# Other places in the scheduler's order for parts of four mixers, and one for each projection

## The chip, the cores and the metric

The kernel runs on one core of a Trainium2 chip. The time is device microseconds of one execution of the whole program; of several runs the median is given.

## What is computed

One layer of a streaming encoder, on 1024 frames of width 1024. A normalised input goes through one input projection whose columns feed four mixers: attention over chunks (A), HGRN2 (H), RWKV-7 (R) and RG-LRU (L). Their outputs are concatenated, projected, normalised and added to the input; an MLP with squared ReLU follows.

```python
h = rms_norm(x, norm_mix_pre[l])
proj = (h @ w_in[l]).astype(f32)
pa, pb, pc, pd = split_cols(proj, [ATTN_COLS, HGRN_COLS, RWKV_COLS, LRU_COLS])
ya = chunk_attention(qa, ka, va, attn_rel_bias[l])
yb = hgrn2(qb, fb, ib, gb, lb_all[l], hgrn_norm[l].astype(f32))
yc = rwkv7(pc, ...)
yd = rglru(xd, gd, ...)
mix = jnp.concatenate([ya, yb, yc, yd], axis=-1).astype(dt)
x = x + rms_norm(mix @ w_out[l], norm_mix_post[l])
h = rms_norm(x, norm_mlp_pre[l])
ff = jnp.square(jax.nn.relu(h @ mlp_w1[l])) @ mlp_w2[l]
x = x + rms_norm(ff, norm_mlp_post[l])
```

## The kernel before

The frames are worked in two halves of 512 (`hf` 0 and 1). Half 0 takes the mixers in the order R, A, L, H, half 1 in the order R, H, A, L (`ORDER`). After them come the output projection of both halves (`out_mm`, L1049 to L1051), the two residuals, and the MLP (from about 730 us on: L1135 to L1137 and L1384 to L1386).

Every float32 product is made from two parts of each operand (`hi` and `lo`), so a projection of 128 columns (`proj_fm`, L318 to L320) is 24 matmuls of 512 columns: eight pieces of depth, three products each. `proj_tm` (L345 to L347) makes a projection of 256 columns the other way round, with 96 matmuls. Each projection loads its weights on SyncE's queue (`wr`, L167), casts the high part on ScalarE (`wh`, L176) and takes the low part on VectorE (`wl`, L178). There are two buffers each of `wr`, `wh` and `wl`, and two PSUM banks with the tag `fm`; a buffer goes to the tiles of its tag in the order of the code, so the projections keep that order whatever their places are, and each needs that the one two ahead of it has been read. A projection's bank comes free when its reader has run (in R the shift, `pcs`, L360, on VectorE). In this text a projection is named by its columns: W_LO, W_K, W_R, W_V of R, A_K, A_Q, A_V of A, L_X and L_G of L, H_F, H_Q, H_I, H_G of H, with j 0 or 1 for the two blocks of 128.

The parts of the mixers that matter here are:

- R. `Rs`: the shifts and gates of both j (with transposes of v into `pv`, L446, copied to `vt` at L448, and sums into `pbon`, L440); `Rc`: 64 by 64 products of be and al into `plt` (L472), copied to `Ld` and `Lo` by ScalarE (L477, L480); `Ri`: the inverse of the 64 by 64 triangles, first steps of 16 on VectorE, then matmuls of 16 (L529, L537, L539) and of 32 (L551, L562) with copies on ScalarE between them; `Rk`, for four blocks of 128 frames: products (L583), then the chain of states (L614 to L651); `Rn`: the end. The bank pair of `plt` is that of L583's `pcp` too.
- H. `Hf`, `Hq`, `Hv`: gates and values; `Hz`, for j 0 and 1: six levels (L776, with copies under a mask on VectorE, L778); `Hs`: the state (L814 to L819) and the output `po` (L825, L832), added up on VectorE (L835).
- A: `Ap` projections, `Ah` the heads. L: `Lx` and `Lg`.

A scheduler orders the instructions of each engine when the program is compiled. It goes through the program as if it ran, and of the instructions that could start on an engine it takes the one with the lowest number; each engine then runs its instructions in that fixed order. The numbers are a count: each instruction takes the next one. `tc.high_priority(offset=n)` starts its block at the count less n and sets the count back at the block's end, so that a block with a place of its own uses up no numbers. Blocks in blocks add up. `at(...)` opens the block of a part of a mixer with n from `PRIO`, `early_by` that of a whole mixer or of the preparation (`p0`, `p1`).

Of the kernel before, what the change touches and what calls it, by code (L numbers as in the profile page):

```python
# [52 lines left out]
NTAIL = 2  # L53
ORDER = ("RALH", "RHAL")

PRIO = {"p1": 130, "R1": 200, "Rs00": 535, "Ah30": 730, "Rs11": 30, "Hq0": 400, "Ah11": 400, "At1": 400,
# [4 lines left out]
LEVELS = (32, 16, 8, 4, 2, 1)  # L61

VEC = {}
# [25 lines left out]
def body(ctx: ExitStack, tc: tile.TileContext, A: dict, out: bass.AP, dbg=None, stop_after=None):  # L89
# [11 lines left out]
    def at(*key):  # L101

        sec.close()
        n = PRIO.get("".join(map(str, key)), 0)
        if n:
            sec.enter_context(tc.high_priority(offset=n))
# [5 lines left out]
    def bank(name, tag="pa"):  # L112
        return psp.tile([P, 512], F32, tag=tag, name=nm(name), bufs=PB[tag])
# [29 lines left out]
    def load_consts():  # L143
        for name, shape in (("cmask", [P, 512]), ("masks", [P, 3 * CH]), ("bones", [P, 2]), ("rkw", [P, 4]),
                            ("lo2", [P, 256]), ("lnw", [P, 256]), ("lnb", [P, 256]), ("hnorm", [P, 256]),
                            ("lgate", [P, 512]), ("lam", [P, 2])):
            consts[name] = load(name, shape, keep)
        lm = ub("lm")[:, 0:6 * CH]
        nc.sync.dma_start(lm, A["lmask"])
        lm8 = keep.tile([P, 6 * CH], mybir.dt.uint8, tag="lm8", name="lm8")  # L150
        V.tensor_copy(lm8[:], lm)
        consts["lmask"] = lm8

        om = keep.tile([P, 25], F32, tag="om", name="om")

        V.tensor_scalar(om[:, 0:7], vecs[:, VEC["mu"]:VEC["mu"] + 7], -1.0, 1.0, MULT, ADD)
        V.tensor_scalar(om[:, 9:11], vecs[:, VEC["k_k"]:VEC["k_k"] + 2], -1.0, None, MULT)

        for i, name in ((13, "bx"), (15, "k_k"), (17, "k_a"), (21, "w0"), (23, "a0")):
            V.tensor_scalar(om[:, i:i + 2], vecs[:, VEC[name]:VEC[name] + 2], 0.5, None, MULT)  # L160
        V.tensor_scalar(om[:, 19:21], om[:, 17:19], -1.0, 1.0, MULT, ADD)
        consts["om"] = om
# [7 lines left out]
    def wload(src, eng=None):  # L170
        return wparts(wraw(src), eng)
# [87 lines left out]
    def spread(hf):  # L259

        rb = bank("rb")
        for t in range(4):
            dg = small.tile([P, P], F32, tag="pdg", name=nm("pdg"))
            V.tensor_scalar(dg[:], ident[:], rs_[hf][:, t:t + 1], None, MULT)
            T.matmul(rb[:, t * P:(t + 1) * P], ones[:], dg[:], start=True, stop=True)
        S.copy(rb_[hf][:], rb[:])

    def prep0():
        nc.sync.dma_start(vecs[:], A["vecs"])
        cols = W_LO, W_K  # L270
        hs, xs, ws = [], [], []
        for k in range(NK):
            xs.append(xload(0, k, lambda s, d, name: hp.tile(s, d, tag="hl", name=name, bufs=NLO)))
            if k < 2:
                ws.append(wraw(wsrc[cols[k]][0]))
        nc.sync.dma_start(ident[:], A["ident"])
        for k, h in enumerate(xs):
            hs.append(parts_in(0, k, h))
            if k < 2:
                early[cols[k]] = wparts(ws[k], (V, G)[k])  # L280
        stats(0)
        proj_pair(hs, *cols)
        spread(0)
        return hs

    def stats(hf):

        ss = small.tile([P, 4, 2], F32, tag="prs", name=nm("prs"))
        for t in range(4):
            for n in range(2):  # L290
                xt = ub("xsq")
                nc.sync.dma_start(xt[:], A["x"][hf * TH + t * P:hf * TH + (t + 1) * P, n * 512:(n + 1) * 512])
                S.activation(xt[:], xt[:], AF.Square, accum_out=ss[:, t, n:n + 1])
        V.tensor_tensor(rs_[hf][:], ss[:, :, 0], ss[:, :, 1], ADD)
        inv_rms(rs_[hf][:], rs_[hf])

    def prep1():
        hs = []
        for k in range(NK):
            h = xload(1, k, lambda s, d, name: hp.tile(s, d, tag="hl", name=name, bufs=NLO))  # L300
            hs.append(parts_in(1, k, h))
        return hs
# [12 lines left out]
    def mm_in(ps, wh, wl, hs, k):  # L315
        hi, lo = hs[k]
        ks = slice(k * P, (k + 1) * P)
        T.matmul(ps[:], wh[:, ks], hi[:], start=(k == 0), stop=False, skip_group_check=True)  # L318
        T.matmul(ps[:], wl[:, ks], hi[:], start=False, stop=False, skip_group_check=True)  # L319
        T.matmul(ps[:], wh[:, ks], lo[:], start=False, stop=(k == NK - 1), skip_group_check=True)  # L320

    def proj_fm(hs, col):

        if col in done:
            return done.pop(col)
        wh, wl = wload(wsrc[col][0])
        ps = bank("fm", "fm")
        for k in range(NK):
            mm_in(ps, wh, wl, hs, k)
        return ps  # L330

    def proj_tm(hs, col):

        pss = [bank("tm", "fm") for _ in range(2)]
        for i, src in enumerate(wsrc[col]):
            wh, wl = wload(src)
            for t in range(4):
                tsl = slice(t * P, (t + 1) * P)
                o = pss[t // 2][:, 256 * (t % 2):256 * (t % 2) + 256]
                for kk in range(4):  # L340
                    k = i * 4 + kk
                    hi, lo = hs[k]
                    cs = slice(kk * 256, (kk + 1) * 256)
                    last = k == NK - 1
                    T.matmul(o, hi[:, tsl], wh[:, cs], start=(k == 0 and t % 2 == 0), stop=False, skip_group_check=True)  # L345
                    T.matmul(o, lo[:, tsl], wh[:, cs], start=False, stop=False, skip_group_check=True)  # L346
                    T.matmul(o, hi[:, tsl], wl[:, cs], start=False, stop=last, skip_group_check=True)  # L347
        return [pss[t // 2][:, 256 * (t % 2):256 * (t % 2) + 256] for t in range(4)]
# [23 lines left out]
    def rwkv(hf, hs):  # L372
        om = consts["om"]
        lo2 = consts["lo2"]
        at("Rs", hf)

        xlo = rwkv_shift(hf, proj_fm(hs, W_LO), 6, "xlo")
        lot = u("lot")
        S.activation(lot[0:32, :], xlo[0:32, :], AF.Tanh)
# [550 lines left out]
    def lru_setup():  # L930

        lam = consts["lam"][:]
        w = [keep.tile([P, 2], F32, name=f"lw{i}") for i in range(4)]
        S.activation(w[0][:], lam, AF.Abs)
        S.activation(w[0][:], w[0][:], AF.Exp, scale=-1.0)
        V.tensor_scalar(w[1][:], w[0][:], 2.0, None, ADD)
        V.reciprocal(w[1][:], w[1][:])
        V.tensor_tensor(w[0][:], w[0][:], w[1][:], MULT)
        V.tensor_tensor(w[1][:], w[0][:], w[0][:], MULT)
        V.memset(w[2][:], 1.0 / 17)  # L940
        for n in (15, 13, 11, 9, 7, 5, 3, 1):
            V.tensor_tensor(w[2][:], w[2][:], w[1][:], MULT)
            V.tensor_scalar(w[2][:], w[2][:], 1.0 / n, None, ADD)
        V.tensor_tensor(w[2][:], w[2][:], w[0][:], MULT)
        V.tensor_scalar(w[3][:], lam, -1.0, 0.0, MULT, MAX)
        V.tensor_scalar(w[2][:], w[2][:], 8.0, None, MULT)
        V.scalar_tensor_tensor(sp8[:, 0:2], w[3][:], 4.0, w[2][:], MULT, ADD)
        V.tensor_scalar(sp8[:, 2:4], sp8[:, 0:2], -1.0, None, MULT)
# [541 lines left out]
    def early_by(n):  # L1490
        return tc.high_priority(offset=n) if n else ExitStack()

    for hf in range(2):
        if hf == 0:
            with early_by(PRIO.get("p0", 0)):
                hs = prep0()
            load_consts()
            for z in zqs + Sbds:
                G.memset(z[:], 0.0)
        else:  # L1500
            with early_by(PRIO.get("p1", 0)):
                hs = prep1()
        for f in ORDER[hf]:
            with early_by(PRIO.get(f + str(hf), 0)):
                {"R": rwkv, "A": attention, "L": lru, "H": hgrn}[f](hf, hs)
                at()
            if f == "R" and hf == 0:
                at("st")
                lru_setup()
                stats(1)  # L1510
                spread(1)
                at()
        if stop_after == f"mix{hf}":
            return
# [84 lines left out]
```

## Time and profile before

| | us |
|---|---|
| median of 3 runs | 1353.74 (1353.53 to 1358.21) |
| profiled execution, time | 1363.41 |
| profiled execution, span | 1361.4 |
| PE busy | 1287.6 (95% of the span) |
| PE weight loads busy | 1017.0 (75%) |
| VectorE busy | 861.6 (63%) |
| ScalarE busy | 662.2 (49%) |
| GpSimd busy | 81.2 (6%) |
| granted TensorE clock, mean | 0.963 of full speed |

The span runs from the first to the last instruction. "Busy" of PE holds time in which the array stands between two matmuls, so 95% doesn't say that it worked at its peak. The granted clock is 1.00 at 2.4 GHz and 0.50 at 1.2 GHz; a stretch between them holds some of both.

### The profile page before, as it was taken

Reading aid. Unit: us, or ns where it says so; the run is one execution under the profiler, and the core shown is the slowest. Engines: PE = TensorE matmul, PEld = TensorE weight load, DVE = VectorE, ACT = ScalarE, POOL = GpSimd, SP = SyncE. Lnnn points to the kernel's source line nnn. Section 1 sums busy time; section 2 is a strip of 40 time slices with the busy share of each in tenths; the row PEclk is TensorE's granted clock in tenths of the full one; section 3 lists DMA queues with packets and bytes.
Section 4 is the critical chain, followed back from the end, with each engine's and each line's share of the span. In section 5 each row is a group of like instructions: output and inputs, shape, how many; then the busy total and the mean of one; then the engine's idle time right before and its main releaser. Section 6 shows DMA issues by size and latency. Waiting matters only on the chain. (4 is left out here: it accounts for less than half of the span.)

```text
span 1361.4 us, 21277 instructions
## 1 busy us (share of the span) xinstructions
PE 1287.6 (95%) x8168; PEld 1017.0 (75%) x8168; DVE 861.6 (63%) x1575; ACT 662.2 (49%) x1171; POOL 81.2 (6%) x123
## 2 busy tenths in 40 slices
PE   6999999899988999999799899999999999999997
PEld 4677778666677777767588678888887888888886
DVE  5653645687463567685648889786774545554884
ACT  6634535565154344574658445444543533433441
POOL 1000010223001123000000000000000000000000
PEclk9998999999688999999899899999998999999999
DMA  8222012311023011235632698787656976556761
GB/s 293 101 92 74 33 61 82 111 61 61 32 81 79 18 39 66 80 122 179 244 126 103 224 312 275 244 267 255 225 174 219 367 253 199 186 187 192 271 231 62
DMA packets 101157, 213.72 MB, mean 157 GB/s; under 512 B 25280, under 2 KB 28992, under 8 KB 101056
## 3 DMA queue, kind: packets, MB, share of 16 engines
q1 hardware_dynamic: 101056, 212.37, 46.1%
q8 instruction: 64, 1.05, 0.3%
q14 instruction: 37, 0.30, 0.1%
HBM read 157.02 MB, written 55.31 MB: 156 GB/s over the span
## 5 line engine op out<-in xcount | busy, mean ns | idle before, releaser
L1384 PE MATMUL q<-b,a 128*128 128x512 f32 x448 | 175.9, 394 | 2.4 <-ACT b L1368 2.4
L1385 PE MATMUL q<-b,a 128*128 128x512 f32 x448 | 176.6, 394 | 0.9 <-DVE b L1369 0.9
L1386 PE MATMUL q<-b,a 128*128 128x512 f32 x448 | 176.3, 393 | 0.0
L318 PE MATMUL fm<-hh,wh 128*128 128x512 f32 x304 | 132.9, 438 | 10.2 <-ACT wh L176 7.6
L319 PE MATMUL fm<-hh,wl 128*128 128x512 f32 x304 | 131.2, 433 | 0.9 <-DVE wl L178 0.9
L320 PE MATMUL fm<-hl,wh 128*128 128x512 f32 x304 | 130.1, 430 | 0.0
L178 DVE TENSOR_TENSOR wl<-wr,wh 128x1024 fp32r<-128x1024 f32 x66 | 82.4, 1249 | 48.4 <-ACT wh L176 47.7
L176 ACT CAST wh<-wr 128x1024 fp32r<-128x1024 f32 x66 | 68.9, 1045 | 87.6 <-PE fm L320 64.9
L1384 PEld LDWEIGHTS q<-b,a 128*128 128x128 f32 x448 | 84.4, 189 | 21.4 <-ACT b L1368 2.8
L1385 PEld LDWEIGHTS q<-b,a 128*128 128x128 f32 x448 | 84.7, 189 | 20.4 <-DVE b L1369 1.7
L1386 PEld LDWEIGHTS q<-b,a 128*128 128x128 f32 x448 | 84.8, 189 | 18.9
L318 PEld LDWEIGHTS fm<-hh,wh 128*128 128x128 f32 x304 | 61.3, 202 | 24.0 <-ACT wh L176 8.3
L1369 DVE TENSOR_TENSOR b<-wb,b 128x1024 fp32r<-128x1024 f32 x32 | 39.1, 1223 | 60.4 <-ACT b L1368 60.2
L319 PEld LDWEIGHTS fm<-hh,wl 128*128 128x128 f32 x304 | 61.3, 202 | 17.4 <-issue 4.3
L320 PEld LDWEIGHTS fm<-hl,wh 128*128 128x128 f32 x304 | 60.8, 200 | 15.0 <-issue 2.6
L1368 ACT CAST b<-wb 128x1024 fp32r<-128x1024 f32 x32 | 33.5, 1048 | 78.7 <-PE q L1385 63.7
L1369 DVE TENSOR_TENSOR a<-ha,a 128x1024 fp32r<-128x1024 f32 x56 | 68.2, 1218 | 5.5 <-ACT a L1368 5.4
L1119 ACT CAST s<-w 128x512 fp32r<-128x512 f32 x64 | 39.3, 619 | 62.4 <-DVE w L1200 16.1
L1369 DVE TENSOR_TENSOR b<-wt,b 128x1024 fp32r<-128x1024 f32 x24 | 29.4, 1224 | 55.9 <-ACT b L1368 55.9
L1368 ACT CAST a<-ha 128x1024 fp32r<-128x1024 f32 x56 | 58.5, 1045 | 7.7 <-DMA ha<-hx 7.7
L1368 ACT CAST b<-wt 128x1024 fp32r<-128x1024 f32 x24 | 25.2, 1049 | 73.5 <-PE q L1385 73.5
L346 PE MATMUL tm<-wh,hl 128*128 128x256 f32 x192 | 55.2, 288 | 0.0
(1082 smaller groups left out, 3045.2 us busy)
## 6 DMA issues: line engine op xcount, KB each, us to landing
ha<-hx SPq DMA_DIRECT2D x56, 512.0 KB, 4.6
wr<-in_win_dram SPq DMA_DIRECT2D x50, 512.0 KB, 3.3
w<-in_w_dram SPq DMA_DIRECT2D x36, 512.0 KB, 5.2
wb<-in_w_dram SPq DMA_DIRECT2D x32, 512.0 KB, 6.6
wt<-tx SPq DMA_DIRECT2D x32, 512.0 KB, 3.7
w2s<-in_w_dram SPq DMA_DIRECT2D x48, 256.0 KB, 4.0
tx<-w2s SPq DMA_DIRECT2D x48, 256.0 KB, 2.4
hx<-h SPq DMA_DIRECT2D x48, 256.0 KB, 3.2
```

Of the source, the lines that this page charges most:

```text
L176: S.copy(hi[:], raw[:])
L178: V.tensor_tensor(lo[:], raw[:], hi[:].bitcast(F32), SUB)
L318: T.matmul(ps[:], wh[:, ks], hi[:], start=(k == 0), stop=False, skip_group_check=True)
L319: T.matmul(ps[:], wl[:, ks], hi[:], start=False, stop=False, skip_group_check=True)
L320: T.matmul(ps[:], wh[:, ks], lo[:], start=False, stop=(k == NK - 1), skip_group_check=True)
L346: T.matmul(o, lo[:, tsl], wh[:, cs], start=False, stop=False, skip_group_check=True)
L1119: S.copy(t[:, 0, :], src)
L1368: S.copy(h_, r[:])
L1369: V.tensor_tensor(l_, r[:], h_.bitcast(F32), SUB)
L1384: T.matmul(o, ah[:, i, tsl], bh[:, i, :], start=start, stop=False, skip_group_check=True)
L1385: T.matmul(o, ah[:, i, tsl], bl[:, i, :], start=False, stop=False, skip_group_check=True)
L1386: T.matmul(o, al[:, i, tsl], bh[:, i, :], start=False, stop=stop, skip_group_check=True)
```

## The change

The table `PRIO` gets other values, and every projection gets a place of its own, under the key "p", its first column, "." and the half.

```diff
+PRIO = {"A0": 30, "Ah01": 400, "Ah10": 100, "Ah11": 400, "Ah20": 60, "Ah21": 260, "Ah30": 730, "At0": 700, "At1": 400,
+        "Hq0": 400, "Hz00": 400, "Hz01": 160, "L0": 30, "L1": 11, "Lg00": 600, "Lg11": 15, "Lx0": 485, "Oh0": 200,
+        "Ol0": 40, "Ol1": 400, "Or0": 400, "Or1": 350, "Pm": 629, "R1": 200, "Ri1": 535, "Rk00": 200, "Rk01": 125,
+        "Rk11": 85, "Rk31": 405, "Rn1": 600, "Rs0": 160, "Rs00": 600, "Rs10": 60, "Rs11": 30, "p0": 800, "p0.1": 196,
+        "p1": 65, "p1536.1": 10, "p2048.1": 10, "p2304.0": 800, "p2688.0": 445, "st": 320}
...
+    half_of = [0]
+
+    def sooner(*key):
+        n = PRIO.get("".join(map(str, key)), 0)
+        return tc.high_priority(offset=n) if n else ExitStack()
+
     def proj_fm(hs, col):
+        with sooner("p", col, ".", half_of[0]):
+            return proj_fm_(hs, col)
+
+    def proj_tm(hs, col):
+        with sooner("p", col, ".", half_of[0]):
+            return proj_tm_(hs, col)
...
     for hf in range(2):
+        half_of[0] = hf
```

The values that differ: p0 none to 800, p1 130 to 65, Rs0 none to 160, Rs00 535 to 600, Rk00 none to 200, st 400 to 320, Lg00 60 to 600, Hs10 30 to none, Hs11 45 to none, Rk01 100 to 125, Rk31 415 to 405, Rn1 200 to 600, L1 none to 11, Ol0 none to 40, Or1 370 to 350; of projections W_V j 0 of half 0 (p2304.0, 800), L_X j 0 of half 0 (p2688.0, 445), A_Q j 0 of half 1 (p0.1, 196), W_K j 0 and H_G of half 1 (p2048.1 and p1536.1, 10 each). No part of the kernel uses "Pm", "At0" or "At1".

What this makes of the numbers, counted along the code by the rule above:

| block | number before | number after |
|---|---|---|
| preparation of half 0 | 15 to 122 | -785 to -678 |
| W_R j 0, half 0 | -345 to -319 | -527 to -501 |
| W_V j 0, half 0 | -307 to -281 | -1289 to -1263 |
| L_X j 1, half 0 | 506 to 532 | 256 to 282 |
| L_G j 0, half 0 | 885 to 911 | 122 to 148 |
| Ri, half 0, its L537 and L539 | 329 to 424 | 212 to 307 |
| Ri, half 0, its L551 and L562 | 431 to 496 | 314 to 379 |
| Hz j 1, half 0 | 1347 to 1426 | 1124 to 1203 |
| Rs j 1, half 1, from its k to its end | 1365 to 1498 | 1190 to 1323 |
| of it the transposes of v, L446 | 1493 to 1496 | 1318 to 1321 |
| Rc, half 1, its copies L477 and L480 | 1427 to 1432 | 1252 to 1257 |
| Hs j 1, half 0, its L825 and L832 | 1433 to 1456 | 1240 to 1263 |
| H_F j 0, half 1, its matmuls | 1430 to 1453 | 1282 to 1305 |
| H_F j 1, half 1, its matmuls | 1460 to 1483 | 1312 to 1335 |
| A_Q j 0, half 1 | 1970 to 1996 | 1602 to 1628 |
| A_K j 0, half 1 | 1942 to 1968 | 1770 to 1796 |
| output projection, half 0 | 2405 to 2638 | 2046 to 2279 |

The matrices, the instructions and their buffers are the same.

## Rows read from the trace of the kernel before

**Rows 1.** The page: TensorE's busy time, and its busy and clock tenths by slice.

```profile
PE 1287.6 (95%) x8168; PEld 1017.0 (75%) x8168; DVE 861.6 (63%) x1575; ACT 662.2 (49%) x1171; POOL 81.2 (6%) x123
PE   6999999899988999999799899999999999999997
PEclk9998999999688999999899899999998999999999
```

**Rows 2.** Stretches by window, start:end first; the columns are in the first row.

```profile
core 0: us, PE busy (x) PEld busy (x) DVE busy (x) ACT busy (x) POOL busy (x), PEclk, DMA share, GB/s
336.00:348.00 12.00, 8.79 (x54) 7.01 (x53) 11.73 (x24) 3.02 (x4) 0.75 (x1) 1.00 0.09 24
476.00:510.00 34.00, 34.00 (x308) 25.30 (x307) 23.42 (x68) 15.43 (x35) 8.31 (x10) 1.00 0.10 34
```

**Rows 3.** Timeline of TensorE, 301 to 373 us: start, duration, line, tiles, count.

```profile
301.14 1.10 PE L825 MATMUL po<-iv,att 128*128 128x64 f32 x8
...
354.21 0.79 PE L320 MATMUL fm<-hl,wh 128*128 128x512 f32 x1
...
361.43 0.79 PE L319 MATMUL fm<-hh,wl 128*128 128x512 f32 x1
362.16 0.47 PE L832 MATMUL po<-sall,qe 64*64 64x64 f32 x2
362.56 0.79 PE L320 MATMUL fm<-hl,wh 128*128 128x512 f32 x1
...
370.75 0.50 PE L318 MATMUL fm<-hh,wh 128*128 128x512 f32 x1
371.19 0.32 PE L832 MATMUL po<-sall,qe 64*64 64x64 f32 x2
371.44 0.50 PE L319 MATMUL fm<-hh,wl 128*128 128x512 f32 x1
...
372.56 0.45 PE L832 MATMUL po<-sall,qe 64*64 64x64 f32 x8
```

**Rows 4.** Stretches by window around that place and behind it.

```profile
350.00:370.00 20.00, 20.00 (x123) 14.17 (x124) 5.02 (x13) 1.89 (x4) 3.10 (x4) 0.50 0.08 27
380.00:385.00 5.00, 0.80 (x17) 0.56 (x19) 2.42 (x3) 4.87 (x9) 0.59 (x2) 0.86 0.16 18
385.00:391.00 6.00, 6.00 (x61) 4.88 (x53) 0.00 (x0) 5.91 (x8) 0.00 (x0) 0.55 0.52 162
394.00:399.00 5.00, 5.00 (x24) 4.14 (x23) 4.79 (x11) 3.42 (x5) 0.00 (x0) 1.00 0.00 0
```

**Rows 5.** Timeline of ScalarE, 354 to 384 us; in brackets idle time before, and its releaser.

```profile
372.67 1.05 ACT L176 CAST wh<-wr 128x1024 fp32r<-128x1024 f32 x1 [17.97 <-PE fm L320]
...
380.58 0.58 ACT L448 COPY vt<-pv 128x512 f32<-128x512 f32 x1
381.06 2.37 ACT L477 COPY Ld<-plt 32x512 f32<-32x512 f32 x4
```

**Rows 6.** Timeline of TensorE, 379 to 385 us.

```profile
379.44 0.60 PE L446 MATMUL pv<-ident,xv 128*128 128x128 f32 x4
...
384.67 0.71 PE L583 MATMUL pcp<-xk,sg 64*64 64x64 f32 x16 [4.21 <-ACT Lo L480]
```

**Rows 7.** Timeline of SyncE's queue, VectorE and TensorE at the start.

```profile
8.23 0.33 SPq L167 DMA_DIRECT2D wr<-in_win_dram  x1
...
24.68 2.35 DVE L178 TENSOR_TENSOR wl<-wr,wh 128x1024 fp32r<-128x1024 f32 x2
...
27.28 0.49 PE L265 MATMUL rb<-pdg,ones 128*128 128x128 f32 x2 [1.98 <-DVE pdg L264]
29.17 0.80 PE L318 MATMUL fm<-hh,wh 128*128 128x512 f32 x1 [1.40 <-DVE pcs L360]
```

**Rows 8.** Stretches by window in R of half 0, during Ri's small matmuls.

```profile
120.00:124.00 4.00, 3.67 (x150) 2.18 (x147) 2.15 (x3) 3.64 (x8) 0.00 (x0) 0.60 0.03 6
124.00:128.00 4.00, 2.67 (x62) 1.66 (x56) 1.22 (x3) 1.84 (x4) 0.95 (x1) 0.50 0.35 131
```

More of the change, by code (lines that the diff above doesn't have):

```diff
@@ L54 @@
 ORDER = ("RALH", "RHAL")
-PRIO = {"p1": 130, "R1": 200, "Rs00": 535, "Ah30": 730, "Rs11": 30, "Hq0": 400, "Ah11": 400, "At1": 400,
[4 rows of a table removed]
+PRIO = {"A0": 30, "Ah01": 400, "Ah10": 100, "Ah11": 400, "Ah20": 60, "Ah21": 260, "Ah30": 730, "At0": 700, "At1": 400,
[4 rows of a table added]
 LEVELS = (32, 16, 8, 4, 2, 1)
@@ L320, in mm_in, with proj_fm_ @@
         T.matmul(ps[:], wh[:, ks], lo[:], start=False, stop=(k == NK - 1), skip_group_check=True)
+    half_of = [0]
+    def sooner(*key):
+        n = PRIO.get("".join(map(str, key)), 0)
+        return tc.high_priority(offset=n) if n else ExitStack()
     def proj_fm(hs, col):
+        with sooner("p", col, ".", half_of[0]):
[3 more added lines that the diff above has]
+            return proj_tm_(hs, col)
+    def proj_fm_(hs, col):
         if col in done:
@@ L330, in proj_fm, with proj_tm_ @@
         return ps
-    def proj_tm(hs, col):
+    def proj_tm_(hs, col):
         pss = [bank("tm", "fm") for _ in range(2)]
```

4 rows, old and new, of the table PRIO are left out of this document.

## The prediction, made before the changed kernel had run

> **What bounds the kernel now.** I read first the page's busy times and its slices. TensorE is busy 1287.6 us, 95% of the span [rows 1]: no change of order can win more than what TensorE idles (74 us), what it loses at a lower clock, and what it loses between matmuls while it counts as busy. All other engines have spare time in every stage. So each edit is asked one thing: does TensorE stand still, run at the lower clock, or change between kinds of matmul less often? The slices say where this can be. From slice 20 on (the output projection and the MLP, about 690 us on) nothing that the change moves is left, but for the order of the loads in front of them. The mixers are the first 17 slices (0 to 590 us), and the clock there is low in slices 3, 10, 11 and 12, worst in 10, at 340 to 374 us, with 0.6 [rows 1]. In most others TensorE is full, as from 476 to 510, 34.00 of 34 us [rows 2]; there an order can only move work about.
>
> I read next the timeline of TensorE in the worst slice. It shows H_F j 0 of half 1 (512 columns, `fm`) taken in turn with the output of Hs j 1 of half 0 (L825, L832): one big, one pair of small ones, one big [rows 3]. From 350 to 370 us TensorE is busy for all 20 us and has the clock of 1.2 GHz, 0.50 [rows 4]. A turn takes 1.13 us there (361.43 to 362.56) and 0.69 us still at full clock (370.75 to 371.44) [rows 3], where big matmuls in a row take about 5.00 / 22, 0.22 us each [rows 4] (24 are in that window, two cut by its ends). The reason is in the table of places: 1430 to 1453 and 1433 to 1456 are the same numbers, and the scheduler merges the two by number.
>
> Third, ScalarE's timeline behind it: it stands idle 17.97 us in front of a cast that waits for H_F's last matmul, and the copies of `plt`, whose matmuls were done at 352, come at 381.06, behind the copy of `pv` (L448) [rows 5]. The transposes that feed that copy run at 379.44, when H_F j 1 is through, and TensorE then idles 4.21 us for `Lo` [rows 6].
>
> **The change part by part.** The shifts in the table come from blocks that no longer use up numbers: 108 of the preparation, 9 of Rs, 106 of Rk (223 in all for what follows in half 0), while Hs j 1 lost its own place and uses up its 75 again (so H of half 1 moves by 148), and 27 of W_K make R's later parts move by 175.
>
> *Hs j 1 against H_F (the main term).* After: 1240 to 1263 against 1282 to 1305. The small ones come first whenever they can run, and H_F runs in one piece beside their waits. From 354.21 to the end of L832 at about 372.9 are 18.7 us [rows 3], with 22 big matmuls, 16 of L825 and 28 of L832. In pieces and at full clock: 22 x 0.22 = 4.8; 16 of L825 at 1.10 per 8 [rows 3], 2.2; 28 of L832 at 0.45 per 8 [rows 3], 1.6; together 8.6 us, so 10.1 less. Its lower end: if the clock stays at 1.2 GHz through, 17.2 us, 1.5 less. After the next idle time, with dense work behind it, 6.0 us had a clock of 0.55 and the stretch from 394 had 1.00 again [rows 4]; that is the nearest row, and such a stretch costs 2.7 us. 10.1 - 2.7: I take 7, between 1.5 and 10.1.
>
> The row shows that a turn of big and small costs more than both in rows of their own. The Trainium skill ("TensorEngine Tiling (Array Packing)", Key Properties) says why: a change of the tiling mode drains TensorE. This trace agrees (0.69 us a turn at full clock, against 0.22 and a share of 0.45 per 8); the sum is the same with or without the rule, but the rule holds as well where the change puts new numbers side by side, which is the second rival.
>
> *The transposes of v.* Numbers 1318 to 1321 now fall into H_F j 1's 1312 to 1335, where they were behind it: about 18 of its 24 matmuls come later, 18 x 0.22 = 4 us earlier for `pv`, and for the `plt` copies behind it. What goes is at most the idle 4.21 us [rows 6] and the slow clock after it, 6 x 0.45 = 2.7 [rows 4], 6.9 together; at least nothing, if the casts of the next projections still stand first on ScalarE. Next late would then be H_Q's cast (L176), which waits for H_F's buffer. I take 2.5.
>
> *The start.* The preparation now comes before the loads and splits of W_R. Before, W_R's load stood ahead of five of the loads of x (8.23 us), two splits on VectorE ran for 2.35 us between `pdg` products, TensorE waited 1.98 us for the last of these and 1.40 us more for `pcs` [rows 7]. W_V, with the lowest number of all, can't pass W_R: buffers go in code order. It can still take VectorE with its one split, 1.2 us. So between 0 and 3.4; I take 2.5. W_V's matmuls will run ahead of W_R's, a swap that pays for itself.
>
> *L_G j 0 and L_X j 1 against Ri.* They go from behind Ri's matmuls to in front of them (122 to 148, 256 to 282). Before, L_G filled the chain of Rk instead. Ri's steps lose 1.66 us idle and, at clocks of 0.60 and 0.50, 1.6 + 2.0 us of speed in 120 to 128 [rows 8]. If the fills cover that, up to 5.3 us less; if L_X takes turns with L537 and L539 (numbers 259 to 282 within 212 to 307), 24 turns of 0.4 us (0.69 less 0.22 less the small one's 0.06) [rows 3, 4], 9.6 us more. L_X's weights were not split in time for this before, and buffers come no sooner now. I take 0.
>
> *At nothing.* p1: the splits of x for half 1 have numbers above Hz and the heads as before; only Hz j 1 has come to stand before them, and it can't start until Hs has given back its bank; cost between 0 and 1. The whole of R in half 1 stands 48 to 75 places later against H of half 0; VectorE is full there (11.73 of 12 us) [rows 2], its sum is unchanged, but readers of banks (L360) wait longer: between -3 and +5, taken at 0, because TensorE has those same projections to do behind it. A_Q before A_K in half 1, st, Rk00, Rk01, Rk31, Rn1: they run where TensorE is full [rows 2], which hides a swap; without that cover each is worth one ScalarE copy and its wait, under 1 us. Ol0, Or1, L1 and the output projection's lower numbers: its operands need buffers that the last projection of L holds, so only splits move, -2 to +2.
>
> Sum: 7 + 2.5 + 2.5 + 0 = 12 us less. In the profiled execution, 1363.4 - 12 = 1351.4; that execution is 9.7 us above the median of the runs, so I set the 12 us against the median: 1353.7 - 12 = **1342 us**.
>
> **The rivals.** *Given back.* The turns go, but the copies of `plt` still stand behind casts on ScalarE and the chain of R starts no earlier; TensorE then runs out of projections sooner and idles longer before L583. Only the start is won: 1353.7 - 2.5 = 1351. For it: ScalarE's 18 us of idle before one cast [rows 5]. Against it: `pv` does move ahead.
>
> *The turns move.* L_X's matmuls merge with L537 and L539 as Hs did with H_F: 1342 + 9.6 = 1352. For it: overlapping numbers. Against it: the weights come late. By the page named above it would happen wherever two tile sizes alternate.
>
> *Slower: Ri runs bare.* If L_G's block ends before the first L537 and L_X is spent in turns with the small ones, the waits of Ri's later steps have no projection left but L_G j 1. From 118 to 138 us, 20 us before, 8 were L_X at mixed clock; 12 remain bare, less 5.3 of L_G j 1, 6.7 idle, and some 3 us of slow clock behind, as in [rows 4]. With the 9.6 of turns: 1342 + 19.3 = 1361. It decides at the point where L_G j 1's first matmul comes after L562. For it: L_G now has a lower number than all of Ri from L537 on. Against it: buffers free up in time for L_G j 1 if L_G is done early.
>
> **How the numbers follow.** Forecast (1342) 0.60, given back (1351) 0.17, turns move (1352) 0.11, slower (1361) 0.12. The measurement of this kernel can tell about 0.5%, 6.8 us, from no change: the first is faster (0.60), the two middle ones are the same (0.28), the last is slower (0.12). The forecast's own bounds: 10.1 + 6.9 + 3.4 + 5.3 = 25.7 us less at best, though not all at once, so 24 is the low end, 1330; the high end takes in both middle cases with some room, 1358. Left out are the slower case (most of its 0.12) and a few hundredths below.
>
> **What would show it.** Right: L825 and L832 in runs of eight and more with no `fm` between them; a clock near 1 within some us of 350; L446 before H_F j 1's end and the idle time before half 1's first L583 under 2 us; the first L318 after `rb` about 2.5 us earlier. Wrong: new turns of L318 to L320 with L537 or L539; a longer idle time before L551, L562 or L583; the same span with the gain of 350 to 373 gone by the start of the output projection.

## The result and the profile after

The changed kernel takes 1333.92 us (1332.13 to 1337.04), the kernel before 1355.97 in the same runs: ratio 0.983, 95% interval 0.980 to 0.986, 22 us less. The profiled execution took 1337.04 us, with a span of 1335.2. In the code of after, the lines behind `proj_fm` stand 14 higher: L360 is L374, L446 is L460, L583 is L597, L825 and L832 are L839 and L846, L1049 is L1063, L1167 is L1181.

The page after, beside [rows 1]: busy times, and TensorE's busy and clock tenths in 40 slices.

```profile
PE 1269.3 (95%) x8168; PEld 1006.3 (75%) x8168; DVE 858.5 (64%) x1575; ACT 665.6 (50%) x1173; POOL 81.9 (6%) x123
PE   6899999899998999989997999999998999999997
PEclk9998999999997999999998999999998999999999
```

TensorE has the same 8168 matmuls and is busy 18.3 us less; it idles 7.9 us less (65.9 for 73.8). The low clock of slices 10 and 11 is gone; slice 12 has 0.7 for 0.8. Windows around H_F of half 1 (start:end; PE, PEld, DVE, ACT, POOL busy; granted clock; DMA), beside [rows 4]:

```profile
330.00:345.00 15.00, 14.59 (x108) 10.51 (x106) 11.43 (x26) 5.12 (x9) 1.49 (x3) 1.00 0.11 38
345.00:361.00 16.00, 15.41 (x141) 12.62 (x140) 8.91 (x15) 8.61 (x15) 3.08 (x4) 1.00 0.33 87
```

The clock is 1.00 throughout. The turns have not all gone: half of L846's matmuls of Hs j 1 still take turns, now with the last projection of R (W_V j 1) instead of H_F (TensorE's timeline: start, duration, line, tiles, count):

```profile
340.32 0.33 PE L846 MATMUL po<-sall,qe 64*64 64x64 f32 x2
340.57 0.51 PE L318 MATMUL fm<-hh,wh 128*128 128x512 f32 x1
341.01 0.33 PE L846 MATMUL po<-sall,qe 64*64 64x64 f32 x2
```

From Hs j 1's first output to its last there are 12 changes between `fm` and `po`, where before has 34. The transposes of v, beside [rows 6], and the first product of Rk behind them (in brackets idle time before and its releaser):

```profile
355.10 0.27 PE L460 MATMUL pv<-ident,xv 128*128 128x128 f32 x1
...
361.04 0.46 PE L597 MATMUL pcp<-xk,sg 64*64 64x64 f32 x16 [0.51 <-ACT Lo L494]
```

They run within H_F j 1 (which ends at 360.3), and the idle time of 4.21 us is 0.51.

Where the time went, by stage, from the first and last matmuls of named tiles in one profiled execution each (us; the last three columns are kernels of the next section):

| stage | before | after | prep_first | three_parts | wv_back |
|---|---|---|---|---|---|
| to W_R's first matmul | 29.2 | 27.3 | 27.6 | 26.9 | 26.2 |
| to the end of A_V, half 0 | 90.4 | 91.1 | 88.1 | 88.0 | 88.0 |
| to the end of H_G, half 0 | 127.6 | 125.2 | 127.3 | 126.8 | 123.8 |
| to the end of H_F j 1, half 1, and Hs j 1, half 0 | 133.3 | 116.7 | 126.6 | 120.8 | 118.1 |
| to the end of the output projection, half 0 | 268.5 | 272.2 | 268.8 | 271.8 | 268.8 |
| to its end, half 1 | 60.3 | 50.7 | 58.6 | 50.2 | 50.7 |

So of the 26 us between the two profiled executions, 16.6 lie where the prediction looked, and 9.6 in the output projection of half 1, where it saw 2 at most; the other stages cancel. Behind it both take 652 us. Each stage holds its execution's share of slow clock: before and prep_first have the same order in the fourth stage and differ by 6.7 us, and after_again, which is after once more, takes 53.1 us for the last stage, not 50.7.

**The clock as a second result.** Every execution has its mean granted clock. Within a kernel, a hundredth of it goes with 10.7 us (the slope over the 180 executions compared here, each kernel's mean taken out; an expectation below was written with 11.7, from fewer of them). It lets the part of a difference that comes with the clock be set aside. Time at a clock of 0.975, and the mean clock:

| kernel | executions | median | mean clock (range) | at 0.975 |
|---|---|---|---|---|
| before | 75 | 1355.7 | 0.968 (0.960 to 0.974) | 1348.9 |
| hs10_sooner | 12 | 1354.2 | 0.969 (0.961 to 0.977) | 1347.8 |
| prep_first | 12 | 1352.5 | 0.969 (0.963 to 0.972) | 1346.0 |
| r_later | 12 | 1350.8 | 0.970 (0.966 to 0.972) | 1344.7 |
| hs10_plain | 6 | 1341.7 | 0.973 (0.964 to 0.976) | 1342.4 |
| prep_and_hs10 | 6 | 1342.6 | 0.973 (0.965 to 0.981) | 1339.7 |
| three_parts | 6 | 1338.3 | 0.979 (0.976 to 0.982) | 1342.0 |
| after, after_again | 10 | 1333.4 | 0.978 (0.974 to 0.979) | 1336.7 |
| shift_back | 11 | 1346.8 | 0.972 (0.963 to 0.979) | 1346.2 |
| lg_back | 6 | 1332.4 | 0.979 (0.975 to 0.981) | 1337.6 |
| out_back | 6 | 1336.6 | 0.976 (0.971 to 0.980) | 1338.4 |
| wv_back | 6 | 1328.5 | 0.981 (0.978 to 0.984) | 1334.6 |
| wv_back_r_later | 12 | 1350.0 | 0.970 (0.963 to 0.976) | 1344.5 |

The last column has a standard error of 0.2 us for before and 0.3 to 0.7 for the others. One execution each of hs10_plain and shift_back, in a slower state of the chip, is left out. Of the 22 us, 12 are there at the same clock, and 0.010 of clock is the other 11.

### The profile page after: what moved, and what is told of

The parts are those of the page before. It is cut to its first block, busy times and chain, and to the rows that moved or that the text cites. A ratio compares the mean times of both kernels' runs of the same rounds, so it can differ in the third digit from the quotient of the medians.

```text
span 1335.2 us, 21293 instructions
## 1 busy us (share of the span) xinstructions
PE 1269.3 (95%) x8168; PEld 1006.3 (75%) x8168; DVE 858.5 (64%) x1575; ACT 665.6 (50%) x1173; POOL 81.9 (6%) x123
## 5 line engine op out<-in xcount | busy, mean ns | idle before, releaser
L318 PE MATMUL fm<-hh,wh 128*128 128x512 f32 x304 | 129.2, 426 | 13.4 <-ACT wh L176 8.9
L319 PE MATMUL fm<-hh,wl 128*128 128x512 f32 x304 | 126.9, 418 | 0.9 <-DVE wl L178 0.9
L320 PE MATMUL fm<-hl,wh 128*128 128x512 f32 x304 | 125.7, 416 | 0.0
L1382 ACT CAST a<-ha 128x1024 fp32r<-128x1024 f32 x56 | 58.6, 1046 | 8.8 <-DMA ha<-hx 8.8
L361 PE MATMUL tm<-wl,hh 128*128 128x256 f32 x192 | 56.0, 292 | 0.6 <-DVE wl L178 0.6
```

The costliest lines, as they stand in the source:

```text
L1382: S.copy(h_, r[:])
```

## The experiments

All compare with runs of the kernel before on the same chip. A number near 1 is the ratio of the times, with its 95% interval in brackets; "in the medians" and "at the same clock" are the columns of the table above. Two theories stood at the outset. "Turns": H_F in turns with the output of Hs j 1 makes the slow clock of 350 to 370 us. "What runs beside Hz j 1": TensorE idles just ahead, the clock falls there, and the turns only lie in the slow stretch.

**hs10_sooner: the tie alone.**

```diff
-"Hs10": 30
+"Hs10": 60
```

> The kernel before with one number of the table changed: Hs j 1 of half 0 gets 60 for 30. Its block uses up no numbers either way, so all else keeps its number; only the tie of L825 and L832 with H_F j 0 of half 1 is gone (1403 to 1426 against 1430 to 1453). Theory 'turns': TensorE changes between big and small matmuls less often and the slow clock of 350 to 370 us goes with it: 5 to 8 us less than before, so about 1349 against 1356. Theory 'what runs beside Hz j 1': the clock falls because TensorE idles beside Hz j 1 just ahead (325 to 349 us), and the turns only come to lie in a stretch that is slow anyway; then the time moves by less than 2 us.

Measured: 0.9989 (0.9968 to 1.0010), 1.1 us less at the same clock. "Turns" falls: of 36 changes between H_F's matmuls and L825 or L832 in the trace of before 13 are left, and hardly anything comes of it. Something else did come with the tie: in this kernel's profile the output projection of half 1 takes 51.0 us with 2.1 idle, as short as in after. Windows of before (first line) and of this kernel where TensorE idles in it:

```profile
660.00:680.00 20.00, 11.78 (x42) 8.40 (x41) 9.87 (x17) 10.87 (x21) 0.00 (x0) 0.76 0.64 229
650.00:660.00 10.00, 9.37 (x44) 7.22 (x43) 5.78 (x11) 7.29 (x19) 0.00 (x0) 1.00 0.95 349
660.00:670.00 10.00, 8.52 (x40) 6.31 (x39) 5.89 (x8) 7.78 (x15) 0.00 (x0) 1.00 0.36 116
```

**prep_first: the start alone.**

```diff
+"p0": 800
```

> The kernel before with p0 800 alone: the preparation of half 0 goes ahead of the loads of R's first projections; all later numbers fall by the same 108, so nothing else changes place. By the prediction 2.5 us less (0 to 3.4), by the traces of before and after 1.5 to 2 us less at W_R's first matmul; a rival: what is won at the start is lost at the next wait, time as before.

Measured: 0.9968 (0.9944 to 0.9991), 3.6 us less in the medians, 2.9 at the same clock: the start as predicted. Its profile says more than was asked. From R's first shifts on, TensorE's instructions stand in the order of before, all the turns with them. Windows, and three lines of TensorE's timeline:

```profile
346.00:352.00 6.00, 6.00 (x34) 4.71 (x31) 2.81 (x10) 1.36 (x3) 0.73 (x2) 0.50 0.00 0
352.00:362.00 10.00, 10.00 (x56) 6.35 (x54) 0.42 (x1) 0.21 (x1) 0.00 (x0) 0.99 0.00 0
```

```profile
352.56 0.33 PE L832 MATMUL po<-sall,qe 64*64 64x64 f32 x2
352.81 0.49 PE L320 MATMUL fm<-hl,wh 128*128 128x512 f32 x1
353.24 0.33 PE L832 MATMUL po<-sall,qe 64*64 64x64 f32 x2
```

The turns run at full clock for 10 us, where before had 0.50 up to 370 us [rows 4]. The clock came back in their midst, so they don't hold it down; the same order took 126.6 us for this stage instead of 133.3. A turn costs 0.68 us at full clock here, as in [rows 3].

**hs10_plain: tie and shift.** Without a place, Hs j 1 uses up 75 numbers, and R of half 1 stands that much later against H of half 0.

```diff
-"Hs10": 30
```

> The kernel before with one entry of the table taken out: Hs j 1 of half 0 has no place of its own and uses up its 75 numbers, so that the tie is gone and R of half 1 with all behind it stands 75 numbers later against H of half 0. Theory 'turns': the same 5 to 8 us less as with the tie alone taken away. Theory 'what runs beside Hz j 1': H of half 0 runs ahead of R of half 1, whose projections are left to fill the waits of Hz j 1, the clock doesn't fall there: 10 to 15 us less than before, and clearly less than with the tie alone taken away.

Measured: 0.9906 (0.9871 to 0.9940), 14 us less in the medians, 6.5 at the same clock, 5.4 more than the tie alone: the number of the second theory. Its reason, that the clock doesn't fall there, did not come: in its profile the clock stays low for longer than in before's (the windows of hs10_plain below).

**r_later: the shift alone, the tie's numbers kept.**

```diff
-"R1": 200
+"R1": 125
```

> The kernel before with the place of R in half 1 at 125 for 200: all of that R stands 75 numbers later against H of half 0, and since its block uses up no numbers nothing else moves; L825 and L832 keep the numbers of H_F j 0 of half 1. Theory 'what runs beside Hz j 1': R's projections are left for the waits of Hz j 1, about 4.5 us less than before at the same granted clock, as the step from the tie alone to tie and shift gave. Rival 'turns': no gain beyond that of fewer turns, 1 to 1.5 us at the same clock.

Measured: 0.9960 (0.9941 to 0.9980), 4.1 us less in the medians and 4.2 at the same clock. The order of R of half 1 against H of half 0 has a price of its own: the turns with H_F are gone here too, but the tie alone gave only 1.1. But the clock is no better (0.970), and its profile shows why that is another matter:

```profile
330.00:337.00 7.00, 2.97 (x16) 2.75 (x16) 5.98 (x9) 0.83 (x3) 0.00 (x0) 0.84 0.23 78
337.00:367.00 30.00, 29.95 (x146) 22.44 (x147) 12.12 (x28) 9.24 (x16) 2.72 (x4) 0.53 0.05 18
```

TensorE idles 4.03 of 7 us beside the last steps of Hz j 1, and then works for 30 us without a break at 0.53.

**shift_back: the changed kernel with the 75 numbers back.**

```diff
+"Hs10": 30
```

> The changed kernel with Hs j 1 of half 0 back at place 30: its 75 numbers are not used up, R of half 1 and all behind it stand 75 numbers sooner again against H of half 0, as before the change. L825 and L832 have the numbers of H_F j 0 again, but H_F runs ahead of them in the compiled order, so that there are few turns (12 changes, with H_F j 1, for 37 before). Theory 'turns': within 3 us of the changed kernel (1334). Theory 'what runs beside Hz j 1': 8 to 12 us above the changed kernel, about 1344, with idle time beside Hz j 1 and a slow clock behind it.

Measured: 1346.84 us, 0.9954 (0.9923 to 0.9984): 13 us above the changed kernel in the medians, 9.5 at the same clock, and the clock down to 0.972. One number undoes more than half of the gain, with few turns in sight. "Turns" had said within 3 us. But the sign that the second theory gave is missing. In two windows of its profile around Hz j 1:

```profile
320.00:330.00 10.00, 9.56 (x49) 6.99 (x50) 9.92 (x22) 5.70 (x11) 2.15 (x3) 1.00 0.01 2
330.00:340.00 10.00, 7.91 (x93) 6.12 (x92) 9.23 (x20) 2.92 (x4) 1.20 (x2) 0.95 0.10 36
```

From Hz j 1's first matmul to Hs j 1's first output TensorE idles 2.5 us, no more than in after (2.8), and the clock is low for 3.4 us up to H_F's end. In the profile the loss lies in the stage up to the end of H_F and Hs j 1 (6.5 us more than after) and in the two stages behind it (1.8 and 2.1). So the number came true, and not by the idle time beside Hz j 1.

**prep_and_hs10 and three_parts: do the parts add up?**

```diff
+"p0": 800
-"Hs10": 30
```

> The kernel before with two of the changes: p0 800, and Hs j 1 of half 0 without a place. If the parts add up, 3.1 (p0) and 5.8 (Hs j 1) us less at the same granted clock, about 1339.7 at 0.975 against 1337 of the changed kernel. Theory 'the clock follows these two': its granted clock is 0.976 or more, as that of the changed kernel, and the median 1336 to 1340. Rival 'the clock has other causes': 0.971 as with Hs j 1 alone, and a median of 1343 to 1346.

Measured: 0.9913 (0.9881 to 0.9946). At the same clock they add up: 2.9 and 6.5 make 9.4, and 1348.9 less 1339.7 is 9.2. The clock doesn't come with them: 0.965 to 0.981, three of six at 0.969 or less. The third part, with the place in the code of after:

```diff
+"p0": 800, "p2048.1": 10
-"Hs10": 30
```

> The kernel before with three of the changes: p0 800, Hs j 1 of half 0 without a place, and the place 10 for W_K j 0 of half 1, which makes R's later parts stand 27 numbers sooner, so 48 instead of 75 later than before. With the first two alone, the last steps of Hz j 1 have no projection beside them (its last 12 matmuls stand in a row, 3.5 to 4 us idle), the clock spreads from 0.965 to 0.981 and the median is 1342.7. With the third, six matmuls of R's last projection (W_LO's j 1, columns 2432) come between them, and the order up to H_F is that of the changed kernel. Theory 'the idle time beside Hz j 1 decides whether the clock falls there': granted clock 0.975 to 0.980 in nearly all runs, median 1335 to 1338, within 3 us of the changed kernel. Rival 'the clock has other causes': clock spread as with two parts, median 1340 to 1343.

(The columns 2432 are W_V j 1; the expectation misnames them.) Measured: 1338.32 us, 0.9851 (0.9815 to 0.9888), and a clock of 0.976 to 0.982 in all six. The median is just above the forecast for it. Windows of the profiled executions of prep_and_hs10 (the first line) and, under it, of three_parts:

```profile
330.00:337.00 7.00, 5.25 (x31) 4.47 (x33) 4.64 (x9) 2.86 (x7) 1.19 (x2) 0.55 0.21 75
```

```profile
330.00:345.00 15.00, 15.00 (x96) 11.09 (x94) 9.94 (x22) 3.85 (x8) 2.19 (x2) 0.77 0.12 38
```

With W_K's place TensorE is without a gap from 330 on, and the idle time in front of Hz j 1's matmuls (the last are L787's) is 2.4 us; without it, no projection stands between the last steps, and it is 4.2. hs10_plain has the order of prep_and_hs10 from R's first shifts on, and in its profile the same gap is followed by 30 us at half clock:

```profile
330.00:337.00 7.00, 3.72 (x19) 3.29 (x18) 5.98 (x9) 2.81 (x6) 0.00 (x0) 0.67 0.21 76
337.00:367.00 30.00, 29.65 (x181) 22.19 (x182) 11.45 (x28) 6.39 (x11) 2.69 (x4) 0.51 0.00 1
```

So the gap gives the clock an occasion to fall; how long it stays down differs between executions of one order (some 7 us here, 30 there). The fourteen profiled executions bear this out: take TensorE's idle time from Hz j 1's first matmul to Hs j 1's first output, and the time at the low clock from that first matmul to the end of H_F. The seven with 3.8 to 5.6 us idle have 6.8 to 34 us of low clock, the seven with 2.4 to 2.8 have 0 to 6.8. In six executions W_K's place went with a steady clock (0.976 to 0.982, for 0.965 to 0.981 without it, on another chip where before ran no faster). That this gap alone does it is not shown: three_parts itself has some 7 us of low clock in its profile, as long as prep_and_hs10, and shift_back has the small gap and W_K's place and spreads from 0.963 to 0.979. At the same clock three_parts is 2.3 us slower than prep_and_hs10, which I did not follow up; in the medians it is 4.3 faster.

**after_again, lg_back, out_back, wv_back: parts of the changed kernel taken back.** after_again is the changed kernel itself.

> The changed kernel itself, for a second profile and more runs with their granted clocks. In the runs so far a hundredth of granted clock goes with 11.7 us; at the same clock (0.975) the changed kernel stands 11 us below the kernel before, and its clock is 0.978 against 0.968, which makes the other 11. Theory 'the clock follows the order': its clock stays at 0.975 to 0.980 in these runs too. Rival 'luck of four runs': the clocks spread from 0.960 to 0.978, as those of the other kernels do, and the median comes out at 1340 or more.

Measured: 1333.01 us, 0.9824 (0.9786 to 0.9862), clock 0.974 to 0.979 in all six. The clock follows the order.

```diff
-"Lg00": 600
+"Lg00": 60
```

> The changed kernel with L_G j 0 of half 0 back at place 60 (its numbers behind Ri and Rk again, L_X j 1's as changed). The prediction took its move at nothing, between 5.3 us less and 9.6 us more; by the trace of after the stretch from A's last projection to the end of H's (118 to 244 us) became 2.4 us shorter. Theory 'L_G fills Ri': 2 to 5 us above the changed kernel. Rival 'order alone': within 1.5 us of it at the same clock.

Measured: 1332.43 us, 0.9820 (0.9781 to 0.9859), 0.9 us more at the same clock than the changed kernel: L_G's move is worth nothing that can be told.

```diff
-"L1": 11, "Ol0": 40, "Or1": 350
+"Or1": 370
```

> The changed kernel with the places of the output's parts as before (no Ol0, no L1, Or1 370). After the mixers the changed kernel gains 9.6 us more up to the MLP: weights for the output projection of half 1 no longer land behind three loads of the MLP's weights. Theory 'heads first': the heads of A end 9 us earlier against the output projection, so the loads of the MLP's weights are through before; then this kernel is within 2 us of the changed one. Rival 'the output's own places': 4 to 8 us above it, with TensorE idle in the output projection of half 1 again.

Measured: 1336.59 us, 0.9849 (0.9810 to 0.9888): 3.6 us above after_again in the medians, 1.7 at the same clock, between the two expectations. In its profile the output projection of half 1 takes 54.4 us with 4.0 idle, for 50.7 with 1.6 in after, 53.1 with 2.5 in after_again and 60.3 with 8.2 before. So the output's own places are the smaller part of the 9.6 us. The rest looks like a matter of the loads. SyncE's queue in before, and under it in after (start, duration of the issues, line, tiles, count):

```profile
657.76 5.14 SPq L1078 DMA_DIRECT2D x1d<-yo  x8
662.96 1.84 SPq L1167 DMA_DIRECT2D w<-in_w_dram  x3
664.84 24.64 SPq L167 DMA_DIRECT2D wr<-in_wout_dram  x5
```

```profile
625.84 2.74 SPq L1181 DMA_DIRECT2D w<-in_w_dram  x3
...
639.27 5.47 SPq L1092 DMA_DIRECT2D x1d<-yo  x8
644.79 17.26 SPq L167 DMA_DIRECT2D wr<-in_wout_dram  x5
```

Before, three loads of the MLP's weights (512 KB each) stand ahead of the next weights of the output projection, which land at 672.5. In after they are out of the way 19 us sooner than those weights. What TensorE waited for, before (line, releaser: us in total, times, longest) and after:

```profile
PE h L1254 <- DVE b1l L1264: 4.5, 2, 2.3
PE po L1050 <- DVE wl L178: 2.0, 1, 2.0
PE po L1049 <- ACT wh L176: 1.7, 1, 1.7
```

```profile
PE po L1063 <- ACT wh L176: 1.0, 1, 1.0
PE h L1268 <- ACT yo L1103: 0.6, 1, 0.6
```

The waits for L1254 are steps that have nothing beside them while the weights are missing. What seems to let the three loads go early is the end of A's last head: it comes 18.8 us before the end of the output projection of half 0 in before, 27.7 in after. Over the fourteen profiled executions, those with 18.8 to 22.4 us take 56.2 to 60.3 for the stage, those with 24.7 or more 50.2 to 54.4. That order of cause is read from the rows and this comparison; no run changes the heads alone. Nor are the 9.6 us that much time won: hs10_sooner has 27.9 us and 51.0 with the tie alone, and is 1.1 us faster at the same clock. What it loses elsewhere for it stays open.

```diff
-"p2304.0": 800
```

> The changed kernel without the place 800 of W_V j 0 in half 0. In after VectorE splits W_V's weights at 27.45 us, ahead of R's first shifts, and TensorE waits 1.76 us in front of W_V's first matmul, which it didn't before. Theory 'the split takes VectorE from the shifts': 1 to 2 us less than the changed kernel. Rival: the wait only moves to W_R's successor, no difference over 0.5 us at the same clock.

Measured: 1328.47 us, 0.9790 (0.9748 to 0.9832), 4.5 us below after_again in the medians and 2.1 at the same clock: the fastest version here. But neither expectation had the place. TensorE's lines with idle time at the start, in after and then in this kernel:

```profile
36.03 0.50 PE L318 MATMUL fm<-hh,wh 128*128 128x512 f32 x1 [1.76 <-DVE pcs L374]
44.37 0.66 PE L440 MATMUL pnb<-ident,nb 128*128 128x128 f32 x4 [1.82 <-ACT nb L438]
```

```profile
35.02 0.50 PE L318 MATMUL fm<-hh,wh 128*128 128x512 f32 x1 [1.76 <-DVE pcs L374]
39.01 0.95 PE L431 MATMUL pss<-bones,sq 128*128 128x2 f32 x8
41.64 0.66 PE L440 MATMUL pnb<-ident,nb 128*128 128x128 f32 x4
```

The wait of 1.76 us at W_V is the same in both. What W_V's place costs is behind it: its 24 matmuls run ahead of the sums of squares (L431, at 41.60 in after, at 39.01 here), on which ScalarE, VectorE and L440 wait, and TensorE idles 1.82 us.

**wv_back_r_later: more of the shift.**

```diff
-"p2304.0": 800
-"R1": 200
+"R1": 125
```

> The changed kernel without W_V's place (1328.5 so far) and with R of half 1 another 75 numbers later (R1 125). Theory 'what runs beside Hz j 1' has no say past the point where the waits of Hz j 1 are filled: in after 2.4 us of idle time are left there, so 0 to 2 us less. Rival 'R too late': R's chain in half 1 starts later and runs out of projections, TensorE idles beside L1049's first or Ri's steps of half 1, 3 to 8 us more.

Measured: 1350.03 us, 0.9962 (0.9936 to 0.9988): 21.6 us worse than wv_back, 9.9 at the same clock, worse than the rival's worst. The idle time beside Hz j 1 is back (4.15 us), the last head ends 22.4 us before the output projection of half 0, and half 1's takes 56.2. 48 numbers later is a good place for R; 123 is not.

## Why the prediction was half right

**The time.** Forecast 12 us less, measured 22; 1333.9 lies within 1330 to 1358, 8 us below the forecast. The direction was right, the size half. That the forecast came this near is in part luck: its largest term (7 of 12) was worth about 1, and terms that it took at nothing brought that back and more.

**Hs j 1 against H_F (7 us, 1.5 to 10.1).** The step that failed is the one from rows to cause: some 8 of the 18.7 us were lost clock (about 16 us of them ran at 0.50 [rows 4]), and I gave them to the turns because they lay together. The tie alone is worth 1.1 us at the same clock, give or take 1.0, about my lower end; prep_first has the same turns at full clock. Nor did the small matmuls come in one piece, as the prediction's first sign asked: half of L832's take turns with R's last projection, at a clock of 1.00. The stage did get 16.6 us shorter in the profile, chiefly because the clock stayed up there.

**R of half 1 later against H of half 0 (taken at 0, between -3 and +5).** This is the term put at nothing that was not. I argued that TensorE has those projections to do behind it anyway. But it is worth 4.2 us at the same clock (r_later, with fewer turns in it), 9.5 in the changed kernel (shift_back). Part of the reason is cover: beside Hz j 1's steps VectorE is the full engine (11.73 of 12 us [rows 2], against the prediction's opening sentence that all other engines have spare time in every stage), TensorE waits for it (L773, L778), and projections of R fill the gaps. The idle time there differs by no more than 3 us between these orders, and shift_back has as little as after; where the rest of the 4.2 and 9.5 us comes from stays open. With W_K's 27 numbers the shift also goes with a higher clock, 0.978 instead of 0.968, 11 us: the gap beside Hz j 1 is one occasion for the clock to fall, and not shown to be all of it.

**The transposes of v (2.5).** As described: idle before Rk from 4.21 to 0.51 us, no slow clock behind it. Its worth was not measured alone.

**The start (2.5, 0 to 3.4).** The preparation's move: 2.9 us (prep_first), with W_R's first matmul 1.6 us earlier in the profile. (W_R's load stood ahead of three of the eight loads of x, not of five.) W_V's place, "a swap that pays for itself", costs 2.1 at the same clock, 4.5 in the medians. Its matmuls did not run ahead of W_R's: W_R's begin at 27.25 us, W_V's at 36.03. I looked for the cost in its split on VectorE, and by the rows it was its matmuls ahead of the small sums.

**L_G and L_X against Ri (0, between -5.3 and +9.6).** Right at 0: lg_back. Neither the turns with L537 and L539 nor the bare Ri came: L_G's matmuls ran between 126.8 and 134.2 us, within Ri, and the last rival's point wasn't reached: L_G j 1 began at 139.4, ahead of L562's matmuls (L576 in after, from 141.2).

**Output projection (-2 to +2).** Wrong for the profile: its half 1 is 9.6 us shorter there. I had looked at the splits, not at the loads that stand ahead of its weights on SyncE's queue, nor at when the heads end. The page had a hint: slice 19 (646 to 680 us) has TensorE at 0.7 [rows 1], and I passed it over, with the output projection put at about 690 us on, where its first matmul is at 588.6. The output's own places are worth 1.7 us at the same clock; what the rest is worth in time stays open, since hs10_sooner has the same short stage for 1.1 us.

**What stays open.** p1, A_Q, H_G, Rs0, Rs00, Rk00, Rk01, Rk31, Rn1, st and L_X were not run alone. three_parts stands 5 us above after; W_V's place is against that and the output's places for it, and the rest is not divided.

## What to carry to other kernels

Before a stretch of slow clock is charged to the work that lies in it, look at what idle time stands just ahead, and at the same stretch in another execution: taking away most of the changes inside was worth 1 us here, and in the profiles the clock fell for longer where the gap was larger. A theory whose number comes true still has to show its sign in the profile: shift_back had the number without the gap. Where blocks of numbers move against each other, ask of every chain with waits which long work remains to stand beside each of its steps, to the last; and of every load moved by it, what is queued ahead. A stage that is shorter in one profile is not yet time won. Compare kernels at the same granted clock as well as by their medians: it showed parts of 2.9 and 6.5 us adding up where the executions spread over 15.

## What the runs showed of the hardware

The granted clock of one order differs between executions: 75 of the kernel before spread from 0.960 to 0.974, some 15 us. At 1.2 GHz TensorE stayed up to 30 us with no gap of note (29.95 of 30 us busy at 0.53), and came back in the midst of alternating tile sizes in another execution.

A turn of one matmul of 512 columns and two of 64 by 64 takes 0.68 us at full clock; apart they are 0.22 and 0.11 [rows 3, 4]. The Trainium skill ("TensorEngine Tiling (Array Packing)", Key Properties) says that a change of tiling mode drains TensorE; this trace agrees with about 0.35 us a turn. Yet 23 changes fewer gave 1.1 us in hs10_sooner, not 11.5 x 0.35 = 4: here the price of a turn was no measure of what taking it away is worth.
